# First operands of an output projection made ahead of the last norm, and weight sums moved from GpSimd to VectorE

## Chip, cores and metric

The kernel runs on one core of one Trainium2 chip. The metric is the device time of one execution in microseconds (us); lower is better. A second, profiled execution gives the trace that the rows below are from.

## Reference

One step of a hybrid layer over 2048 prompt tokens and 64 sample tokens (8 sequences of 8), model width 1024, float32. The normed input goes through one projection; three head groups (an SSD scan, gated linear attention, sliding-window attention) each give a part of a 1024-wide mix; the mix goes through `w_out`, and a gated embedding is added. What matters here is the end:

```python
y = (y.reshape(Bsz, L, SSD_WIDTH) * jax.nn.silu(z))
y_ssd = rmsnorm(y.reshape(Bsz, L, 2, 256), ssd_norm_w.reshape(2, -1)).reshape(Bsz, L, SSD_WIDTH)
...
mix = jnp.concatenate([y_ssd, y_gla, y_swa], axis=-1) @ w_out      # 512 + 256 + 256 -> 1024
h = h + mix
h = h + jax.nn.sigmoid(h @ w_pg) * (p @ w_pe)
```

## The kernel before

**Stages.** Tokens are 16 tiles of 128 in 8 blocks of 256; the 64 sample tokens make a 17th tile. Linear attention, window attention and the SSD come first, with tokens in the free dimension; the SSD norm of a block (`s_norm`, L1297 to L1317) is the last thing that its mix needs. Mixes are stored to DRAM (`mixd0` to `mixd16`) and come back in the output stage ("o", L1487 on). The gate stage ("g") follows it.

**Products.** Float32 is kept by splitting each operand into two fp32r parts, high (ScalarE, L1505) and low (VectorE, L1506), with three matmuls for a product of blocks. The output stage takes tiles in pairs and multiplies the 256x1024 mix of a pair by the 1024x1024 `w_out` in the manner of Strassen: seven products a pair, P1 A11·B11, P6 S2·T2, P7 S3·T3, P5 S1·T1, P4 A22·T4, P2 A12·B21, P3 S4·B22, each of 12 matmuls of 128x128 by 128x512. The sample tile alone is a group of four (P1, P6, P2, P3). There are nine groups (pair 0, sample, pairs 1 to 7): 60 products. A11, A12, A21, A22 are quarters of the mix, S1 to S4 their sums (L1563 to L1574: on VectorE for pair 0, on GpSimd for the others). A11 and A21 are the SSD halves, the part that waits for the norm; pair 0 is of block 0, whose norm is long done. Its operands S3, S1 and A22, however, lie in box X9, which the last block's SSD values hold (X_S in the trace) until they are stored to `mixd14` and `mixd15`. Products end in four PSUM banks: X (P1, P2), Y (P6), Z (P7, P4), V (P5, P3); the sums with the residual `h` are at L1534 and L1535 and at L1585, on GpSimd for the sum of P1 and P6 (three adds of 128x512 a group), on VectorE otherwise. A bank's second product starts when the add of its first has read it.

**Weight sums.** T1 to T4 are sums of quarters of `w_out` (and of `w_pg` for the gate), made ahead and kept in DRAM: `t_sums` (L1394 to L1413) goes through eight rounds, each four loads of 128x256 (tile `quads`), four subtractions on GpSimd (L1405, L1406, L1408, L1409; tile `sums`) and four stores (`gT`, `oT`). For `w_pg` this runs beside the output stage.

**What sets the order.** `class Order` lists the work for all engines in advance. Dense units (`od.unit`) keep their order; the generators in `od.chain` are stepped whenever their time is due by the figures that they yield (cost, latency) or by the table `LAT`. Each engine then takes its instructions in the order of that list, except that the scheduler behind it moves them a little. SyncE issues all loads and stores in one row, and a store there that waits for its data holds what is behind it. `c_second` (L1731) loads `h` of the first two groups and makes S3, S1 and A22 of pair 0; `c_weights` (L1476) loads and splits the weights of `w_out`; `last_weights` does B22. All tiles of a phase share boxes of memory named in its plan (`Phase`, L943 for the SSD).

Of the kernel before, what the change touches and what calls it, by code (L numbers as in the profile page):

```python
# [12 lines left out]
AF = mybir.ActivationFunctionType  # L13
# [136 lines left out]
def hybrid_step(ctx: ExitStack, tc: tile.TileContext, I, C, O):  # L150
# [780 lines left out]
    def swa_tiles(odd):  # L931
# [12 lines left out]
        xr1 xr2 xr3:X8; sones afs:Y0; xc:Y0 X9; par2 cdp decs:Y0; sst0 sst1 sst2 sst3 cio:Y1; S0s:Y1 Y1; ab:Y2 Y2; zs rr:Y2;  # L944
# [167 lines left out]
    def u_z(b, m):  # L1112
# [8 lines left out]
        V.scalar_tensor_tensor(out=zss[b][:, m], in0=th[:, 0], scalar=1.0, in1=pf, op0=ALU.add, op1=ALU.mult)  # L1121
        if m == 3:
            od.mark(("z", b), 0.8)
            used(2 * NB + b)
            if b == NB - 1:
                c_weights(2)
# [170 lines left out]
    def s_norm(b):  # L1297
        n = ncols(b)
        yield 0, 0, ("z", b), *[("ch", t[0]) for t in tiles_of(b)]
        y, zs = xcs[b][:, 0:4], zss[b]  # L1300
        V.tensor_tensor(out=y, in0=y, in1=zs, op=ALU.mult)
        A.activation(out=zs, in_=y, func=AF.Square)
        G.tensor_tensor(out=zs[:, 0:4:2], in0=zs[:, 0:4:2], in1=zs[:, 1:4:2], op=ALU.add)
        rr = s1.tile([128, 2, n], F32, tag="rr", name="rr")
        yield 0.9 if n == 256 else 1.1, LAT["y2"] if b < NB - 1 else 3.0
# [88 lines left out]
    def t_sums(w, pause, *needs):  # L1394

        yield 0, 0, *needs
        for k in range(4):
            for c in (0, 256):
# [138 lines left out]
    class Out(Square):  # L1537
# [39 lines left out]
        def unit(self, g, n):  # L1577
# [26 lines left out]
            if G_[0] in self.h:  # L1604
                adds()
            else:
                self.late.append(adds)
# [136 lines left out]
    seq = [(0, 0), (0, 1), (1, 0), (0, 5), (1, 1), (0, 2), (0, 3), (0, 4), (1, 2), (0, 6), (1, 3)]  # L1744
# [121 lines left out]
```

## Time and profile before

| | us |
|---|---|
| median of three runs | 1233.59 (1233.57, 1233.59, 1239.47) |
| profiled execution | 1243.2 |
| its span (first to last instruction) | 1241.4 |
| PE busy | 1181.1 (95%) |
| VectorE busy (DVE) | 711.8 (57%) |
| ScalarE busy (ACT) | 484.2 (39%) |
| GpSimd busy (POOL) | 464.6 (37%) |

The profiled execution lies 9.6 us above the median. Busy shares are means over unlike stages; the stage that the change works in is the output stage, from 812.7 to 1003.9 us of the span, with the gate stage behind it to the end.

### The profile page before, as it was taken

Reading aid. Unit: us, or ns where it says so; the run is one execution under the profiler, and the core shown is the slowest. Engines: PE = TensorE matmul, PEld = TensorE weight load, DVE = VectorE, ACT = ScalarE, POOL = GpSimd, SP = SyncE. Lnnn points to the kernel's source line nnn. Section 1 sums busy time; section 2 is a strip of 40 time slices with the busy share of each in tenths; the row PEclk is TensorE's granted clock in tenths of the full one; section 3 lists DMA queues with packets and bytes.
Section 4 is the critical chain, followed back from the end, with each engine's and each line's share of the span. In section 5 each row is a group of like instructions: output and inputs, shape, how many; then the busy total and the mean of one; then the engine's idle time right before and its main releaser. Section 6 shows DMA issues by size and latency. Waiting matters only on the chain.

```text
span 1241.4 us, 20938 instructions
## 1 busy us (share of the span) xinstructions
PE 1181.1 (95%) x8010; PEld 991.3 (80%) x8010; DVE 711.8 (57%) x1442; ACT 484.2 (39%) x993; POOL 464.6 (37%) x537
## 2 busy tenths in 40 slices
PE   7899999998999998999899999889998999999998
PEld 6787887687888887988798988757776878688886
DVE  4665565745544356568666658866745674344552
ACT  4443433542344346333345535453222352233331
POOL 4222324214411124436334444334877323333331
PEclk8899999999999999998999999999999999999999
DMA  8645465285632256422512343456677432322221
GB/s 251 224 173 191 153 238 160 72 253 158 211 120 99 86 179 200 170 74 80 172 60 95 120 136 112 152 174 202 210 260 261 153 128 70 102 77 77 87 83 51
DMA packets 119036, 182.33 MB, mean 147 GB/s; under 512 B 35573, under 2 KB 88293, under 8 KB 112792
## 3 DMA queue, kind: packets, MB, share of 16 engines
q1 hardware_dynamic: 118936, 180.99, 44.2%
q8 instruction: 63, 1.03, 0.3%
q14 instruction: 37, 0.30, 0.1%
HBM read 125.59 MB, written 55.37 MB: 146 GB/s over the span
## 4 chain that ended last, share of the span: by engine, by line
PE 58%; DMA 14%; DVE 11%; ACT 5%; POOL 4%; issue 4%; SPq 3%; POOLq 0%; DVEq 0%; ACTq 0%
PE pT L205 9%; PE pg L205 5%; PE pfz L205 5%; PE pfx L205 4%; PE pXg L1529 4%; PE peC L205 4%; PE pVg L1529 4%; PE pZg L1529 3%; PE po L205 2%; PE pq L205 2%; PE pYg L1529 2%; DMA quads<-in_w_pg_dram 2%; PE pys L205 2%; DMA raw<-in_w_in_dram 1%; DMA Y_S<-afd 1%
## 5 line engine op out<-in xcount | busy, mean ns | idle before, releaser
L205 PE MATMUL pfx<-uh,w 128*128 128x256 f32 (+1 forms) x768 | 153.1, 294 | 3.8 <-ACT X_S L1094 2.5
L205 PEld LDWEIGHTS pfx<-uh,w 128*128 128x128 f32 x768 | 123.8, 193 | 8.7 <-ACT X_S L1094 3.2
L205 PE MATMUL pfx<-ul,w 128*128 128x256 f32 (+1 forms) x384 | 111.0, 289 | 0.0
L205 PE MATMUL pfz<-uh,w 128*128 128x256 f32 (+1 forms) x512 | 105.4, 298 | 4.2 <-DVE Y_S L1121 3.4
L205 PE MATMUL pg<-uh,w 128*128 128x256 f32 (+1 forms) x512 | 103.4, 294 | 1.6 <-DVE Y_W L891 1.6
L1683 POOL TENSOR_TENSOR X_C<-ul_D,X_C 128x512 f32<-128x512 f32 (+1 forms) x33 | 43.0, 1303 | 135.5 <-DVE ul_D L1682 112.0
L205 PEld LDWEIGHTS pfz<-uh,w 128*128 128x128 f32 x512 | 84.8, 197 | 7.1 <-DVE Y_S L1121 4.2
L205 PE MATMUL pT<-w,uh 128*128 128x512 f32 (+1 forms) x272 | 87.9, 400 | 0.0
L205 PEld LDWEIGHTS pg<-uh,w 128*128 128x128 f32 x512 | 83.2, 193 | 4.6 <-DVE Y_W L891 2.2
L205 PE MATMUL pfz<-ul,w 128*128 128x256 f32 (+1 forms) x256 | 75.4, 294 | 0.0
L205 PEld LDWEIGHTS pfx<-ul,w 128*128 128x128 f32 x384 | 74.0, 193 | 1.5 <-issue 1.3
L205 PE MATMUL pg<-ul,w 128*128 128x256 f32 (+1 forms) x256 | 74.9, 293 | 0.0
L205 PE MATMUL pT<-Y_G,uh 128*128 128x280 f32 (+1 forms) x272 | 62.7, 314 | 3.8 <-ACT uh L326 3.5
L229 DVE TENSOR_TENSOR w<-raw,w 128x1024 fp32r<-128x1024 f32 x32 | 46.6, 1466 | 27.4 <-ACT w L227 27.3
L227 ACT ACTIVATE w<-raw 128x1024 fp32r<-128x1024 f32 x40 | 41.6, 1056 | 49.8 <-DMA raw<-in_w_in_dram 21.5
L205 PEld LDWEIGHTS pT<-w,uh 128*128 128x128 f32 (+1 forms) x272 | 48.8, 185 | 12.1 <-issue 1.8
L1506 DVE TENSOR_TENSOR uh_C<-ul_C,uh_C 128x512 fp32r<-128x512 f32 (+1 forms) x35 | 33.5, 967 | 39.9 <-ACT uh_C L1505 39.9
L1682 DVE SCALAR_TENSOR_TENSOR ul_D<-ul_D,peC 128x512 f32<-128x512 f32 (+1 forms) x34 | 23.3, 685 | 54.1 <-PE peC L205 46.1
L1529 PE MATMUL pZo<-w,X_C 128*128 128x512 f32 x192 | 48.3, 401 | 6.0 <-DVE X_C L1585 6.0
L205 PE MATMUL pT<-w,ul 128*128 128x512 f32 (+1 forms) x136 | 53.9, 397 | 0.0
L205 PE MATMUL peC<-Y_P,uh_C 128*128 128x512 f32 (+1 forms) x204 | 52.8, 393 | 0.8 <-DVE ul_D L1682 0.8
L1505 ACT ACTIVATE uh_C<-ul_C 128x512 fp32r<-128x512 f32 (+1 forms) x35 | 20.8, 609 | 81.2 <-POOL ul_C L1574 31.2
(437 smaller groups left out, 3045.5 us busy)
## 6 DMA issues: line engine op xcount, KB each, us to landing
uh<-uhd SPq DMA_DIRECT2D x14, 1024.0 KB
ul<-uld SPq DMA_DIRECT2D x14, 1024.0 KB
raw<-in_w_in_dram SPq DMA_DIRECT2D x17, 512.0 KB
X_G<-in_x_prompt_dram SPq DMA_DIRECT2D x16, 512.0 KB
Y_S<-afd SPq DMA_DIRECT2D x16, 512.0 KB
X_C<-in_x_prompt_dram SPq DMA_DIRECT2D x16, 512.0 KB
ul_C<-mixd SPq DMA_DIRECT2D x16, 512.0 KB
out_y_prompt_dram<-X_C SPq DMA_DIRECT2D x16, 512.0 KB
```

The lines of the kernel that those rows point to most:

```text
L205: PE.matmul(out, lhsT=lhsT, rhs=rhs, start=start, stop=stop)
L227: A.activation(out=hi[:, k0:k1], in_=rw, func=AF.Copy, scale=scale)
L229: eng.tensor_tensor(out=lo[:, k0:k1], in0=rw, in1=hi[:, k0:k1].bitcast(F32), op=ALU.subtract)
L1505: A.activation(out=t[:, 0, :, :R], in_=src, func=AF.Copy)
L1506: eng.tensor_tensor(out=t[:, 1, :, :R], in0=src, in1=t[:, 0, :, :R].bitcast(F32), op=ALU.subtract)
L1529: PE.matmul(ps[:R], lhsT=a[:, x, k, :R], rhs=b[:, y + k], start=first and k + i == 0, stop=k == 3 and i == 2, skip_group_check=True)
L1682: V.scalar_tensor_tensor(out=th, in0=th, scalar=1.0, in1=pe[:R], op0=ALU.add, op1=ALU.mult)
L1683: eng.tensor_tensor(out=h[:R, cs], in0=th, in1=h[:R, cs], op=ALU.add)
```

## The change

- In the SSD's plan the two boxes of `xc` change places, so that the last block's values lie in Y0 and the block before that in X9.
- The norm of the last block takes its product with the gate and its squares in two halves, the first after two of the four z units; the second half's sum of squares goes from GpSimd to VectorE. The planner's latency of the norm falls from 6.9 and 3.0 to 2.5 for the last two blocks.
- `c_second` stands right behind the last z unit and needs only the end of the scan. It takes the loads of T1 and T4 along, which stood in the last z unit.
- The first eleven products stand in another order, and the operands of group 2 are made in two parts.
- The sums of `w_pg` go from GpSimd to VectorE, and from a chain with due times to steps taken at fixed products: 34 steps, one after each product of groups 2 to 6 but the first (four steps a round), with no condition on their end but an assertion.

```diff
-        xr1 xr2 xr3:X8; sones afs:Y0; xc:Y0 X9; par2 cdp decs:Y0; sst0 sst1 sst2 sst3 cio:Y1; S0s:Y1 Y1; ab:Y2 Y2; zs rr:Y2;
+        xr1 xr2 xr3:X8; sones afs:Y0; xc:X9 Y0; par2 cdp decs:Y0; sst0 sst1 sst2 sst3 cio:Y1; S0s:Y1 Y1; ab:Y2 Y2; zs rr:Y2;
...
+        if m == 1:
+            od.mark(("z1", b), 0.8)
         if m == 3:
             od.mark(("z", b), 0.8)
             used(2 * NB + b)
-            if b == NB - 1:
-                c_weights(2)
...
-        yield 0, 0, ("z", b), *[("ch", t[0]) for t in tiles_of(b)]
-        y, zs = xcs[b][:, 0:4], zss[b]
-        V.tensor_tensor(out=y, in0=y, in1=zs, op=ALU.mult)
-        A.activation(out=zs, in_=y, func=AF.Square)
-        G.tensor_tensor(out=zs[:, 0:4:2], in0=zs[:, 0:4:2], in1=zs[:, 1:4:2], op=ALU.add)
+
+        for i, m in enumerate((2, 4) if b == NB - 1 else (4,)):
+            last = m == 4
+            yield 0, 0, ("z" if last else "z1", b), *[("ch", t[0]) for t in tiles_of(b)]
+            y, zs = xcs[b][:, 0:4], zss[b]
+            h = slice(2 * i, m)
+            V.tensor_tensor(out=y[:, h], in0=y[:, h], in1=zs[:, h], op=ALU.mult)
+            A.activation(out=zs[:, h], in_=y[:, h], func=AF.Square)
+            (V if i else G).tensor_tensor(out=zs[:, 2 * i:m:2], in0=zs[:, 2 * i:m:2], in1=zs[:, 2 * i + 1:m:2], op=ALU.add)
         rr = s1.tile([128, 2, n], F32, tag="rr", name="rr")
-        yield 0.9 if n == 256 else 1.1, LAT["y2"] if b < NB - 1 else 3.0
+        yield 0.9 if n == 256 else 1.1, LAT["y2"] if b < NB - 2 else 2.5
...
-                yield 0, pause
+                yield
+                yield
                 t = stg.tile([128, 4, 256], F32, tag="raw", name="sums")
-                G.tensor_tensor(out=t[:, 0], in0=q[:, 1], in1=q[:, 0], op=ALU.subtract)
-                G.tensor_tensor(out=t[:, 1], in0=q[:, 3], in1=t[:, 0], op=ALU.subtract)
-                yield 0, 2.5
-                G.tensor_tensor(out=t[:, 2], in0=q[:, 3], in1=q[:, 1], op=ALU.subtract)
-                G.tensor_tensor(out=t[:, 3], in0=q[:, 2], in1=t[:, 1], op=ALU.subtract)
-                yield 0, pause - 3.0
+                E.tensor_tensor(out=t[:, 0], in0=q[:, 1], in1=q[:, 0], op=ALU.subtract)
+                E.tensor_tensor(out=t[:, 1], in0=q[:, 3], in1=t[:, 0], op=ALU.subtract)
+                yield
+                E.tensor_tensor(out=t[:, 2], in0=q[:, 3], in1=q[:, 1], op=ALU.subtract)
+                E.tensor_tensor(out=t[:, 3], in0=q[:, 2], in1=t[:, 1], op=ALU.subtract)
+                yield
...
-seq = [(0, 0), (0, 1), (1, 0), (0, 5), (1, 1), (0, 2), (0, 3), (0, 4), (1, 2), (0, 6), (1, 3)]
+seq = [(0, 0), (0, 1), (0, 2), (0, 5), (1, 0), (1, 1), (0, 3), (0, 4), (0, 6), (1, 2), (1, 3)]
...
-preps = {(0, 0): "1 A11", (0, 5): "1 A12", (0, 6): "1 S4", (0, 4): "2 A11 S2 S3 S1 A22", (1, 2): "2 A12", (1, 3): "2 S4"}
+preps = {(0, 0): "1 A11", (0, 5): "1 A12", (0, 6): "1 S4", (1, 1): "2 A11 S2", (0, 4): "2 S3 S1 A22", (1, 2): "2 A12", (1, 3): "2 S4"}
+
+gs = t_sums("g", V)
...
         if (g, n) == (2, 0):
             e_weights()
-            od.mark("summing", 6.0)
+        elif 2 <= g < last - 1:
+            next(gs, None)
...
+            if n == 0:
+                assert next(gs, "end") == "end"
             operand("g", *late[n])
 
     od.unit(0, c_mid, ("U", 3 * NB - 1))
+    od.unit(0, c_second, "ssd")
     for g, n in seq:
-        od.unit(2.73, partial(o_unit, g, n), ("o", co.prods(g)[n][2]), *([("sums", "g")] if g == last else []))
-        if (g, n) == (0, 5):
-            od.unit(0, c_second, ("norm", NB - 1), "ssd", "cstate")
+        od.unit(2.73, partial(o_unit, g, n), ("o", co.prods(g)[n][2]))
```

How the rows of the engines move, at three places. In these rows a name is box, phase and a number (`X9_C`: box X9, output stage; `_S`: SSD), then the shape; the lines of the changed kernel are ten further on in the output stage, four to five in the SSD.

**The last norm and pair 0's operands.** VectorE, before: the last norm's final step is L1312; L1506 on X9_C is the low part of S3, S1 and A22.

```order
L1585 TENSOR_TENSOR X7_C_8878<-pXo_8826,X7_C_8878 64x512
L1506 TENSOR_TENSOR uh_C_8787<-ul_C_8592,uh_C_8787 128x512
L1312 SCALAR_TENSOR_TENSOR X9_S_5228<-X9_S_5228,Y0_S_3525,Y2_S_5188 128x256 x4
L1535 TENSOR_TENSOR ul_C_8785<-ul_C_8785,pYo_8893 64x512
L1506 TENSOR_TENSOR uh_C_8595<-ul_C_8592,uh_C_8595 128x512
L229 TENSOR_TENSOR Y2_C_8863<-raw_8864,Y2_C_8863 128x1024
L229 TENSOR_TENSOR Y2_C_8863<-raw_8868,Y2_C_8863 128x1024
L1506 TENSOR_TENSOR X9_C_8884<-ul_C_8592,X9_C_8884 128x512 x3
```

VectorE, after (L1305 is the norm's product, in halves; L1316 its final step; L1516 on X9_C the low parts):

```order
L1305 TENSOR_TENSOR Y0_S_3525<-Y0_S_3525,Y2_S_5189 128x512
L1290 COPY Y2_S_5189<-ptf_8694 128x256
L1516 TENSOR_TENSOR X9_C_8801<-ul_C_8592,X9_C_8801 128x512
L1331 COPY Y2_S_5189<-ptx_8737 3x384
L1516 TENSOR_TENSOR X9_C_8801<-ul_C_8592,X9_C_8801 128x512 x2
L1121 SCALAR_TENSOR_TENSOR Y2_S_5189<-X6_S_5154,pfz_8707 128x256
L1331 COPY Y2_S_5189<-ptx_8702 3x384
L229 TENSOR_TENSOR w512_8783<-raw_8784,w512_8783 128x1024
L229 TENSOR_TENSOR w512_8783<-raw_8788,w512_8783 128x1024
L1121 SCALAR_TENSOR_TENSOR Y2_S_5189<-X7_S_5196,pfz_8743 128x256
L1516 TENSOR_TENSOR uh_C_8772<-ul_C_8592,uh_C_8772 128x512
L1305 TENSOR_TENSOR Y0_S_3525<-Y0_S_3525,Y2_S_5189 128x512
```

The low parts of S3, S1 and A22 (X9_C) stood behind the norm's last step and stand now ahead of the norm's second half, among the z units (L1121).

SyncE at the same place, before (`mixd16` is the sample mix, in `ul_C`):

```order
L1315 DMA mixd12_115<-Y0_S_3525 128x4x128
L1315 DMA mixd13_116<-Y0_S_3525 128x4x128
L1293 DMA out_ssm_prompt_dram<-Y2_S_5188 128x64 x4
L1543 DMA ul_C_8785<-mixd16_119 128x8x64
L1499 DMA X6_C_8875<-in_x_prompt_dram 128x1024 x2
L1543 DMA ul_C_8785<-mixd5_108 128x1024
L226 DMA raw_8771<-oT4_216 128x1024
```

SyncE, after:

```order
L1319 DMA mixd12_115<-X9_S_5081 128x4x128
L1319 DMA mixd13_116<-X9_S_5081 128x4x128
L1293 DMA out_ssm_prompt_dram<-Y2_S_5189 128x64 x4
L1553 DMA ul_C_8592<-mixd3_106 128x1024
L1509 DMA X6_C_8778<-in_x_prompt_dram 128x1024
L1332 DMA out_conv_prompt_dram<-Y2_S_5189 3x768
L1553 DMA ul_C_8770<-mixd16_119 128x8x64
```

The load of the sample mix stood right behind the final state's stores; now the load of `mixd3` (into the buffer that S3, S1 and A22 are made from), a load of `h` and a store of the convolution state are ahead of it.

**The first products.** PE, before, from the end of the last z unit (`pXo`, `pYo`, `pZo`, `pVo`: the four banks; 64x512: the sample group; `pn`: the last norm's sum over partitions):

```order
L1529 MATMUL pXo_8793<-w512_8155,uh_C_8595 128x512 x12
L1529 MATMUL pYo_8811<-w512_8394,uh_C_8595 128x512 x12
L1529 MATMUL pXo_8793<-Y1_C_8164,uh_C_8787 128x512 x2
L1529 MATMUL pXo_8826<-w512_8155,uh_C_8595 64x512 x2
L1529 MATMUL pXo_8793<-Y1_C_8164,uh_C_8787 128x512 x10
L1529 MATMUL pXo_8826<-w512_8155,uh_C_8595 64x512 x10
L1529 MATMUL pXo_8826<-Y1_C_8164,uh_C_8787 64x512 x12
L205 MATMUL pn_8839<-Y2_S_5188,Y0_S_3525 128x512
L1529 MATMUL pYo_8893<-w512_8394,uh_C_8595 64x512 x12
L1529 MATMUL pXo_9018<-w512_8155,uh_C_8595 128x512 x12
L1529 MATMUL pZo_8909<-w512_8403,X9_C_8884 128x512 x2
```

PE, after:

```order
L1539 MATMUL pYo_8828<-w512_8394,uh_C_8595 128x512 x12
L1539 MATMUL pXo_8810<-w512_8155,uh_C_8595 128x512 x12
L1539 MATMUL pXo_8897<-w512_8155,uh_C_8595 64x512 x12
L1539 MATMUL pXo_8810<-Y1_C_8164,uh_C_8772 128x512 x3
L205 MATMUL pn_8846<-Y2_S_5189,Y0_S_3525 128x512
L1539 MATMUL pZo_8856<-w512_8403,X9_C_8801 128x512 x12
L1539 MATMUL pXo_8810<-Y1_C_8164,uh_C_8772 128x512 x9
L1539 MATMUL pYo_8910<-w512_8394,uh_C_8595 64x512 x12
L1539 MATMUL pVo_8933<-w512_8783,X9_C_8801 128x512 x12
L1539 MATMUL pZo_8856<-w512_8792,X9_C_8801 128x512 x12
L1539 MATMUL pXo_8897<-Y1_C_8164,uh_C_8772 64x512 x12
```

Ahead of `pn` stand now P6, P1 and the start of P2 of pair 0 and the sample's P1, and P7 of pair 0 (`pZo`) right behind it, with P5 and P4 three products later. Before, P7 of pair 0 stood behind P1 and P2 of both groups, `pn`, the sample's P6 and group 2's P1.

**The weight sums.** GpSimd, before, at the first rounds (L1405 to L1409 the sums; L1563 to L1574 sums of the mix; L1585 adds to `h`):

```order
L1405 TENSOR_TENSOR sums_9155<-quads_9102 128x256
L1408 TENSOR_TENSOR sums_9155<-quads_9102 128x256
L1565 TENSOR_TENSOR ul_C_8592<-ul_C_8592 128x512
L1406 TENSOR_TENSOR sums_9155<-quads_9102,sums_9155 128x256
L1574 TENSOR_TENSOR ul_C_8592<-ul_C_8592 128x512
L1563 TENSOR_TENSOR ul_C_8592<-ul_C_8785 128x512
L1409 TENSOR_TENSOR sums_9155<-quads_9102,sums_9155 128x256
L1564 TENSOR_TENSOR ul_C_8785<-ul_C_8785 128x512
L1565 TENSOR_TENSOR ul_C_8785<-ul_C_8592,ul_C_8785 128x512
L1585 TENSOR_TENSOR X6_C_8875<-ul_C_8785,X6_C_8875 128x512 x2
L1405 TENSOR_TENSOR sums_9274<-quads_9222 128x256
```

VectorE, after, at two of the later rounds (L1410 to L1414 the same sums):

```order
L1595 TENSOR_TENSOR X6_C_8778<-pZo_9367,X6_C_8778 128x512
L1516 TENSOR_TENSOR X9_C_8801<-ul_C_8770,X9_C_8801 128x512
L1410 TENSOR_TENSOR sums_9608<-quads_9571 128x256
L1595 TENSOR_TENSOR X6_C_8778<-pVo_9385,X6_C_8778 128x512
L1516 TENSOR_TENSOR X9_C_8801<-ul_C_8592,X9_C_8801 128x512
L1411 TENSOR_TENSOR sums_9608<-quads_9571,sums_9608 128x256
L1413 TENSOR_TENSOR sums_9608<-quads_9571 128x256
L1414 TENSOR_TENSOR sums_9608<-quads_9571,sums_9608 128x256
L1595 TENSOR_TENSOR X6_C_8778<-pZo_9367,X6_C_8778 128x512
L1410 TENSOR_TENSOR sums_9696<-quads_9659 128x256
L1595 TENSOR_TENSOR X6_C_8778<-pXo_9322,X6_C_8778 128x512
```

The four subtractions of a round left GpSimd, whose rows in these groups are now L1573 to L1584 and L1595 alone, and stand on VectorE between the adds that free the banks (L1595) and the low parts (L1516).

## Rows read from the trace of the kernel before

**Rows 1.** Windows: stretch, us, busy of PE, PEld, DVE, ACT, POOL, granted clock, DMA share, GB/s.
```profile
812.70:1003.90 191.20, 174.10 (x740) 136.61 (x738) 115.18 (x134) 62.36 (x93) 110.52 (x88) 0.97 0.64 212
812.70:867.00 54.30, 46.80 (x185) 33.12 (x183) 33.73 (x39) 22.56 (x31) 22.11 (x16) 0.94 0.63 197
867.00:1003.90 136.90, 127.29 (x556) 103.49 (x555) 81.45 (x95) 39.80 (x62) 88.41 (x72) 0.99 0.65 217
1003.90:1241.00 237.10, 230.10 (x1081) 184.67 (x1079) 109.16 (x166) 71.76 (x130) 74.91 (x58) 1.00 0.24 82
```
**Rows 2.** Waits of PE, 805 to 1005 us: total us, times, longest us.
```profile
PE pZo L1529 <- DVE X_C L1585: 6.0, 3, 3.0
PE pXo L1529 <- ACT ul_C L1534: 4.1, 2, 2.9
PE pYo L1529 <- DVE uh_C L1506: 2.3, 1, 2.3
```
**Rows 3.** Timeline of PE: start, us, what, matmuls [idle before <- releaser].
```profile
812.74 3.00 PE L1529 MATMUL pXo<-w,uh_C 128*128 128x512 f32 x12
...
828.33 4.22 PE L1529 MATMUL pXo<-Y_C,uh_C 128*64 128x512 f32 x12 [2.91 <-ACT ul_C L1534]
832.35 1.42 PE L205 MATMUL pn<-Y_S 128*128 128x512 f32 x2
833.20 3.09 PE L1529 MATMUL pYo<-w,uh_C 128*64 128x512 f32 x11
...
867.03 2.88 PE L1529 MATMUL pVo<-w,X_C 128*128 128x512 f32 x12
869.75 2.88 PE L1529 MATMUL pXo<-w,uh_C 128*128 128x512 f32 x12
...
955.20 4.61 PE L1529 MATMUL pZo<-w,X_C 128*128 128x512 f32 x12 [2.99 <-DVE X_C L1585]
```
**Rows 4.** Timeline of SyncE's queue, ScalarE and VectorE about the last norm.
```profile
814.79 0.58 SPq L1543 DMA_DIRECT2D ul_C<-mixd  x1
...
818.67 0.42 ACT L1505 ACTIVATE uh_C<-ul_C 128x256 fp32r<-128x256 f32 x1 [3.30 <-DMA ul_C<-mixd]
...
836.77 1.67 DVE L1312 SCALAR_TENSOR_TENSOR X_S<-X_S,Y_S 128x256 f32<-128x256 f32 x4 [2.90 <-ACT Y_S L1310]
...
841.76 1.67 ACT L1505 ACTIVATE X_C<-ul_C 128x512 fp32r<-128x512 f32 x3 [1.15 <-DMA mixd<-X_S]
```
**Rows 5.** Chain of waits, 780 to 1010 us: start, us, what.
```profile
818.02 8.70 DMA raw<-oT
...
885.86 4.65 DMA quads<-in_w_pg_dram
```
**Rows 6.** Windows around two stalls of PE, columns as in rows 1.
```profile
837.00:842.00 5.00, 3.05 (x8) 2.14 (x9) 4.95 (x8) 2.50 (x4) 1.66 (x1) 0.80 0.34 105
953.00:958.00 5.00, 2.80 (x8) 2.29 (x9) 4.46 (x5) 1.98 (x4) 4.36 (x3) 0.80 1.00 371
```
**Rows 7.** Waits of GpSimd and VectorE, 805 to 1005 us.
```profile
POOL sums L1405 <- DMA quads<-in_w_pg_dram: 12.9, 5, 4.6
...
DVE X_C L1585 <- POOL X_C L1585: 6.6, 2, 5.2
```
**Rows 8.** Groups by line and shape, 867 to 970 us: busy us, mean ns | idle before.
```profile
L1585 POOL TENSOR_TENSOR X_C<-ul_C,X_C 128x512 f32<-128x512 f32 x16 | 25.0, 1585 | 1.0 <-DVE ul_C L1535 1.0
...
L1406 POOL TENSOR_TENSOR sums<-quads,sums 128x256 f32<-128x256 f32 x7 | 6.9, 984 | 2.6 <-DMA quads<-in_w_pg_dram 2.6
```
**Rows 9.** Timeline of VectorE and GpSimd: VectorE alone, and beside GpSimd.
```profile
799.15 0.69 DVE L1563 TENSOR_TENSOR ul_C<-ul_C 128x512 f32<-128x512 f32 x1
...
801.03 1.29 POOL L1163 TENSOR_TENSOR X_S<-X_S 128x512 f32<-128x512 f32 x1 [2.50 <-DMA X_S<-ead]
801.50 1.37 DVE L1564 TENSOR_TENSOR ul_C<-ul_C 128x512 f32<-128x512 f32 x1
...
860.67 0.41 DVE L1506 TENSOR_TENSOR uh_C<-ul_C,uh_C 128x256 fp32r<-128x256 f32 x1
```

More of the change, by code (lines that the diff above doesn't have):

```diff
@@ L1392, in hybrid_step, with t_sums @@
     t_d = {(w, t): tc.dram_tile([128, 4, 512], F32, name=f"{w}{t}") for w in "og" for t in ("T1", "T2", "T3", "T4")}
-    def t_sums(w, pause, *needs):
-        yield 0, 0, *needs
+    def t_sums(w, E):
+        t = None
         for k in range(4):
@@ L1402, in t_sums, with o_sums @@
                         SP.dma_start(out=q[ps, i], in_=s)
-                yield 0, pause
+                yield
+                yield
                 t = stg.tile([128, 4, 256], F32, tag="raw", name="sums")
-                G.tensor_tensor(out=t[:, 0], in0=q[:, 1], in1=q[:, 0], op=ALU.subtract)
-                G.tensor_tensor(out=t[:, 1], in0=q[:, 3], in1=t[:, 0], op=ALU.subtract)
-                yield 0, 2.5
-                G.tensor_tensor(out=t[:, 2], in0=q[:, 3], in1=q[:, 1], op=ALU.subtract)
-                G.tensor_tensor(out=t[:, 3], in0=q[:, 2], in1=t[:, 1], op=ALU.subtract)
-                yield 0, pause - 3.0
+                E.tensor_tensor(out=t[:, 0], in0=q[:, 1], in1=q[:, 0], op=ALU.subtract)
[4 more added lines that the diff above has]
+                yield
                 for i in range(4):
                     SP.dma_start(out=t_d[w, f"T{i + 1}"][:, k, c:c + 256], in_=t[:, i])
-        od.mark(("sums", w))
+    def o_sums():
+        yield 0, 0, "wg", ("qk", 0)
+        for i, _ in enumerate(t_sums("o", G)):
+            yield 0, (5.5, 5.5, 2.5, 8.0)[i % 4]
+        od.mark(("sums", "o"))
     ws = {}
@@ L1486, in __init__ @@
         def __init__(self, w, groups, sets):
-            self.w, self.groups, self.sets, self.late = w, groups, sets, []
+            self.w, self.groups, self.sets = w, groups, sets
             self.mx, self.h, self.op, self.ps, self.pt, self.r = {}, {}, {}, {}, {}, {}
@@ L1602, in adds @@
                     SP.dma_start(out=h_d[i][:R], in_=self.h[i][:R])
[L1604 to L1607, printed above, removed]
+            adds()
             if g > 1:
@@ L1733, in c_second @@
         co.load_h(1)
-        for f in co.late:
-            f()
+        c_weights(2)
         for key in ("S3", "S1", "A22"):
@@ L1780, in hybrid_step @@
             od.unit(3.5, partial(cg.unit, g, n), ("g", cg.prods(g)[n][2]))
-    od.chain(t_sums("o", 11.0, "wg", ("qk", 0)))
-    od.chain(t_sums("g", 6.0, "summing"))
+    od.chain(o_sums())
     od.chain(last_weights())
```

## Prediction

> **What bounds the kernel now.** I read the windows first. From 812.7 us on the kernel is the output stage (191.2 us to the first gate product) and the gate stage (237.1 us) [rows 1]. In the gate stage PE is busy 230.1 of 237.1 us, so what the output stage saves or loses reaches the end. Next the timeline of PE: undisturbed products start 2.72 us apart (867.03, 869.75) [rows 3], and 60 of them would take 163.2 us. The stage takes 191.1, so 28 us are lost in it. Third, where: the first 15 products end at 867.0, 54.3 us for 40.8, 13.5 lost; the other 45 take 136.9 for 122.4, 14.5 lost [rows 1, 3]. Of these, idle PE is 54.3 - 46.8 = 7.5 and 136.9 - 127.3 = 9.6 [rows 1]; the rest is products that ran longer. Fourth, the waits of PE say who is waited for: the adds that free banks Z (6.0) and X (4.1), and an operand's low part (2.3) [rows 2]. After each such wait the granted clock is 0.80 over five us [rows 6]: part of the stretch at 1.2 GHz instead of 2.4. A window of 5 us at 0.80 has lost 5 x 0.20 = 1.0 us, and a product right behind a wait took 4.22 or 4.61 in place of 3.00 [rows 3]. So a wait costs itself and 1.0 to 1.6 more.
>
> **Head: what goes.** Before, pair 0's P7 cannot start until S3 is made, and S3 lies where the last block's SSD values lie. The last norm's step ends at 838.4, its store must have read them, and the copies of S3, S1 and A22 start at 841.8 [rows 4], 29 us into the stage. PE meanwhile has only P1, P2 and P6 of both groups, and waits between them, since two products share bank X (2.91 at 828.33) [rows 3]. The change gives the last block's values another box, so S3, S1 and A22 depend on the block before, whose norm is done during the z units; their rows stand ahead of the last norm's second half. P7, P5 and P4 can fill the gaps, and no operand of pair 0 is late. This is the edit with one answer: the 13.5 us are the pot.
>
> **Head: what is late next.** On SyncE the sample mix's load now stands behind the load of mixd3, which waits until VectorE has read S3, S1 and A22 from its buffer, and behind a load of h and a store that waits for VectorE. Before, it was issued at 814.79, and the sample's A11 began at 818.67, 3.9 us later [rows 4]. After, I set its issue at 815 to 816, about a z unit later, so A11's high part (0.42) and low part are ready at 820 to 821.3. PE has P6 and P1 of pair 0 first and comes to the sample's P1 at 812.74 + 2 x 2.72 = 818.2. It waits 1.9 to 3.1; I take 2.5. Bounds: 1 if SyncE gets through faster, 4 if the convolution store (its data come from VectorE) holds it. Nothing can pass, as PE goes in order. Behind the wait the clock costs 1.0 to 1.6, I take 1.5. The norm's matmuls `pn` stay: 0.85 from their start to the next product's (832.35 to 833.20) [rows 3]. Together 4.9 lost where 13.5 were: **8.6 gained**, between 13.5 - 0.85 - 1.0 = 11.7 (wait of 1, no clock loss) and 13.5 - 0.85 - 4 - 1.6 - 2 = 5.0, where the last 2 stand for a late T4 or pn. T4's load, second half, lands at 826.7 before [rows 5]; its place on SyncE hardly moves and its split takes some 3 us more, while P4 stands ninth on PE and cannot start before 812.74 + 8 x 2.72 = 834.5. B22 is needed later still. So these are covered by 5 us or more. The norm in halves and the sum on VectorE shorten a chain that nobody waits for any more (block 7's mix is needed in the last group); their cost is nothing while that holds, and if pn were late PE would stand, which the 2 covers.
>
> **The other groups: what goes.** Of the 9.6 idle, 2.3 is group 2's operand S2, late because of the head [rows 2]; its operands are now begun two products earlier. 6.0 is bank Z's add [rows 2]. Its releaser is VectorE's add, which is itself behind GpSimd's three adds to the same h (6.6 in two waits), and GpSimd is held by the weight sums: its subtractions wait 12.9 us for the quads [rows 7]. A longest case of 2.99 at 955.20 [rows 3] is a load of h queued on SyncE behind stores of the sums, which wait for GpSimd. With the sums off GpSimd, all four subtractions of a round (four of about 0.98 [rows 8], 3.9 us) and their waits leave it; in this stretch it is busy 88.4 of 136.9 us [rows 1], and the 32 subtractions are 31 of these 88. The h adds (1.585 each [rows 8]) then follow P6 at once. The remaining 1.3 (9.6 - 6.0 - 2.3) is at the turn to the gate and stays. So 8.3 idle can go, and with three waits 1.0 each of clock: 11.3 at most.
>
> **The other groups: what comes.** VectorE gets 32 subtractions of 128x256. One such operation took 0.41 alone [rows 9], 13 us in all; it has 136.9 - 81.5 = 55 us free [rows 1]. Beside GpSimd the same 128x512 operation took 1.37, alone 0.69 [rows 9]; doubled, the 32 take 26 us, and still fit. What does not fit as easily is order: VectorE takes its rows in turn, so a subtraction that waits for its quads holds the bank's add behind it. On GpSimd such waits were 12.9 in five, 2.6 in the mean and 4.6 at most [rows 7]; the loads themselves take 4.65 [rows 5]. In the new order they are issued two products (5.4 us) ahead of their use, so most are in. I take one wait that reaches PE, 2.6 and 1.0 of clock, and 0.9 that is left of the late h load, whose queue still has the stores in it. **Gain 11.3 - 4.5 = 6.8**, between 0 (four such waits, or the next rival) and 11.3. The condition on the sums ahead of the last group is gone from the list, which costs nothing: the last step stands at the last round's product.
>
> The Trainium skill speaks against this edit: "SBUF — State Buffer", section "Who interferes with whom", says that a VectorE instruction with two SBUF inputs and a GpSimd instruction that reads SBUF exclude each other, so that one is blocked until the other ends. The trace agrees so far as it goes: 1.37 beside GpSimd against 0.69 [rows 9]. By it VectorE would not be given GpSimd's time for nothing.
>
> **Sum.** The profiled run took 1243.2 (span 1241.4 and 1.8 around it); 8.6 + 6.8 = 15.4 makes 1227.8. The median is 9.6 below the profiled run; I take it that both lose the same in these stalls, so the median becomes 1233.6 - 15.4 = **1218.2, say 1218**. The other phases (813 us) keep their order but for boxes and the earlier norm of block 6, and I cost them at nothing: the first write into the new boxes waits for VectorE work that is long done.
>
> **Rivals.** (A) All of it hides: no new wait in the head but pn, none from the quads. 1233.6 - 11.7 - 11.3 = 1210.6, with one wait left about 1212. For it: products are issued with two products of slack. Against: SyncE's order is there to be read, and the sample's load is in it.
>
> (B) VectorE and GpSimd block each other. If each of the 32 subtractions waits for a GpSimd operation of 0.98 [rows 8], they take 32 x 1.4 = 45 us of VectorE's 55 free, and GpSimd is held in turn; adds of banks come late again and the later groups gain nothing: 1233.6 - 8.6 = 1225.0 (1224 to 1227). For it: the pair in [rows 9]. Against: GpSimd would then be busy 57 of 137 us, so that most subtractions meet nothing.
>
> (C) The 9.6 us by which the profiled run is above the median lie in these very stalls, so that a usual run has less to save: 15.4 - 9.6 = 5.8, 1227.8; or the sample's load takes 4 and more and the steady gain is 0: 1233.6 - 5.0 = 1228.6. Against the first: most of these waits follow from the order of instructions, which is the same in each run.
>
> (D) Slower: VectorE is held in each of eight rounds by quads, as GpSimd was, with an add for PE behind it. By the longest wait, 8 x 4.6 = 36.9 [rows 7]: 1233.6 - 15.4 + 36.9 = 1255. It decides from (15.4 + 6.2) / 8 = 2.7 us a round reaching PE. For it: DMA is at 0.65 busy in this stretch and at 1.00 around 955 [rows 1, 6]. Against: the loads are issued two products ahead, GpSimd's chain issued them as its due times came, and PE's banks allow one product of delay.
>
> **How the numbers follow.** 0.5% (6.2 us) is about what a measurement of this kernel can tell from no change. Forecast, 1212 to 1224: 0.50. A, 1209 to 1212: 0.10. B, 1224 to 1227.4: 0.16. C, 1227.4 to 1234: 0.16. D, over 1239.8: 0.08, of which little lies below. Faster (under 1227.4) is 0.50 + 0.10 + 0.16 = 0.76, same 0.16, slower 0.08. The range leaves out D, half of A and a part of C: 1211 to 1229.
>
> **What would show it.** In the changed profile: the copies of S3, S1 and A22 start before 815, not at 841.8; PE's first wait in the stage is for the sample's A11, about 2.5 at 818; 15 products take some 46 us instead of 54.3. In the later groups no row of sums is left on GpSimd, PE's waits for bank Z's add fall from 6.0 to under 3, VectorE shows waits for quads, and the stage takes about 176 us. Wrong would be: a wait for T4 or pn in the head, subtractions well over 1 us on VectorE with PE waiting for adds, or more than 2.7 us of PE's waits a round behind quads.

## The result, and the profile after

| | before | changed |
|---|---|---|
| median, 14 runs each (us) | 1237.65 | 1227.34 |
| profiled execution, span (us) | 1241.4 | 1222.0 |
| ahead of the output stage (us) | 812.7 | 803.3 |
| output stage, first product to first gate product (us) | 191.1 | 181.0 |
| of it the first 15 products / the other 45 (us) | 54.3 / 136.8 | 44.8 / 136.2 |
| gate stage, to the end of the span (us) | 237.6 | 237.7 |

The ratio of the times is 0.9915, 95% interval 0.9889 to 0.9941: 7.3 to 13.7 us faster, where 15.4 were forecast. The time lies in the stated range. The median of before is now 4 us above that of the three runs which the forecast started from. The spans differ by 19.4 us, of which 9.5 lie ahead of the output stage. A second profile of the changed kernel reaches its output stage at 808.4, so that part moves between executions of one program, and I don't count it. The stage itself is 10.1 us shorter; the second profile has 179.9. So differences of about 1 us between stages, each of one profile, say nothing.

Windows of the changed kernel (stretch, us, busy of PE, PEld, DVE, ACT, POOL, clock, DMA share, GB/s; PE is TensorE's matmuls, PEld its weight loads), to be laid beside [rows 1]:

```profile
803.20:984.30 181.10, 169.47 (x739) 134.94 (x739) 121.16 (x164) 60.11 (x89) 84.08 (x55) 0.99 0.68 221
803.20:848.00 44.80, 42.60 (x185) 31.69 (x185) 32.47 (x45) 21.94 (x31) 22.80 (x14) 1.00 0.80 258
848.00:984.30 136.30, 126.87 (x555) 103.25 (x555) 88.69 (x120) 38.17 (x58) 61.29 (x42) 0.99 0.64 209
```

The head (the first 15 products) is 9.5 us shorter and its granted clock is at 1.00 instead of 0.94. In the other 45 products GpSimd is busy 61 us instead of 88 and VectorE 89 instead of 81, as meant, but PE is idle 9.4 us instead of 9.6: nearly nothing is gained there. The timeline of PE says where it stands, with [rows 3] beside it:

```profile
803.26 2.91 PE L1539 MATMUL pYo<-w,uh_C 128*128 128x512 f32 x12
...
810.36 0.68 PE L1539 MATMUL pXo<-w,uh_C 128*64 128x512 f32 x2 [1.47 <-ACT uh_C L1515]
811.77 2.50 PE L1539 MATMUL pXo<-w,uh_C 128*64 128x512 f32 x10 [0.73 <-DVE uh_C L1516]
...
815.26 3.31 PE L1539 MATMUL pZo<-w,X_C 128*128 128x512 f32 x12
...
845.32 2.88 PE L1539 MATMUL pVo<-w,X_C 128*128 128x512 f32 x12
...
853.46 3.02 PE L1539 MATMUL pZo<-w,X_C 128*128 128x512 f32 x12 [2.54 <-DVE X_C L1595]
...
875.97 4.54 PE L1539 MATMUL pZo<-w,X_C 128*128 128x512 f32 x12 [3.62 <-DVE X_C L1595]
```

P7 of pair 0 (pZo, 815.26) starts 12.0 us into the stage, where it stood at 30.9. The only wait of the head is the sample's P1, 1.47 + 0.73 = 2.2 us. In the later groups come waits for bank Z's add as before, now 2.54 and 3.62; the wait for S2, 2.3 before, is gone, and 1.8 for bank V came.

Waits of PE and VectorE in the changed kernel, 800 to 986 us (total, times, longest); the third row answers to the first of [rows 7]:

```profile
PE pZo L1539 <- DVE X_C L1595: 6.2, 2, 3.6
...
PE pVo L1539 <- DVE X_C L1595: 1.8, 2, 1.4
...
DVE sums L1410 <- DMA quads<-in_w_pg_dram: 17.8, 6, 6.2
```

GpSimd's wait for the quads, 12.9 us, is now VectorE's, 17.8 us, and bank Z's wait is 6.2 where it was 6.0 [rows 2]. How the one makes the other, in the timelines of VectorE and GpSimd:

```profile
871.13 0.43 DVE L1410 TENSOR_TENSOR sums<-quads 128x256 f32<-128x256 f32 x1 [6.16 <-DMA quads<-in_w_pg_dram]
...
872.79 0.68 DVE L1545 TENSOR_TENSOR ul_C<-ul_C,pYo 128x512 f32<-128x512 f32 x1
...
873.55 4.56 POOL L1595 TENSOR_TENSOR X_C<-ul_C,X_C 128x512 f32<-128x512 f32 x3 [7.15 <-DVE ul_C L1545]
...
875.23 0.69 DVE L1595 TENSOR_TENSOR X_C<-pZo,X_C 128x512 f32<-128x512 f32 x1 [1.15 <-POOL X_C L1595]
```

VectorE stands 6.16 us before a subtraction. Behind it in its row is L1545, the sum of banks X and Y, for which GpSimd's three adds to h wait 7.15; behind the first of these is bank Z's add, and PE's 3.62.

### The profile page after: what moved, and what is told of

Its sections match the earlier page's. It is cut to its first block, busy times and chain, and to the rows that moved or that the text cites. A ratio compares the mean times of both kernels' runs of the same rounds, so it can differ in the third digit from the quotient of the medians.

```text
span 1222.0 us, 20943 instructions
## 1 busy us (share of the span) xinstructions
PE 1168.4 (96%) x8010; PEld 983.9 (81%) x8010; DVE 720.3 (59%) x1476; ACT 484.4 (40%) x994; POOL 441.8 (36%) x505
## 5 line engine op out<-in xcount | busy, mean ns | idle before, releaser
L205 PE MATMUL pfz<-uh,w 128*128 128x256 f32 (+1 forms) x512 | 102.8, 293 | 3.9 <-DVE Y_S L1121 2.5
L205 PEld LDWEIGHTS pfz<-uh,w 128*128 128x128 f32 x512 | 82.3, 191 | 7.0 <-DVE Y_S L1121 3.3
L1689 DVE SCALAR_TENSOR_TENSOR ul_D<-ul_D,peC 128x512 f32<-128x512 f32 (+1 forms) x34 | 23.3, 685 | 53.7 <-PE peC L205 48.1
L205 PEld LDWEIGHTS pT<-Y_G,uh 128*128 128x128 f32 (+1 forms) x272 | 46.2, 197 | 7.5 <-ACT uh L326 3.6
L205 PEld LDWEIGHTS pg<-ul,w 128*128 128x128 f32 x256 | 49.3, 193 | 0.9 <-issue 0.4
```

Of the source, the lines that this page charges most:

```text
L205: PE.matmul(out, lhsT=lhsT, rhs=rhs, start=start, stop=stop)
L1689: V.scalar_tensor_tensor(out=th, in0=th, scalar=1.0, in1=pe[:R], op0=ALU.add, op1=ALU.mult)
```

## Experiments

Each kernel was timed in five rounds beside the kernel before. The stage is that of its one profile, from the first product to the first gate product; the last column splits it where 15 products are done. "Head alone" is the changed kernel with the sums of `w_pg` left on GpSimd as before. The times tell the large steps apart; differences of 0.3% between the versions near 0.99 lie within their intervals, and there the stage and its waits are read. The first 15 products run from 43.9 to 48.1 us in kernels with the same head, by the clock behind one wait, so that the sums are judged by the other 45.

| kernel | ratio (95%) | stage | first 15 / other 45 |
|---|---|---|---|
| changed, second profile | 0.9905 (0.9873 to 0.9938) | 179.9 | 44.0 / 136.0 |
| head alone | 0.9878 (0.9844 to 0.9912) | 176.7 | 46.2 / 130.5 |
| sums alone | 1.0019 (0.9998 to 1.0041) | 193.4 | 57.4 / 136.0 |
| sums at fixed products, on GpSimd | 0.9888 (0.9854 to 0.9922) | 176.6 | 43.9 / 132.7 |
| one product more of slack | 0.9891 (0.9855 to 0.9927) | 179.0 | 44.1 / 135.0 |
| head alone, old order | 0.9891 (0.9860 to 0.9923) | 177.5 | 45.7 / 131.8 |
| head alone, old boxes | 0.9998 (0.9974 to 1.0023) | 187.4 | 55.1 / 132.3 |
| changed, no quads read | 0.9917 (0.9892 to 0.9943) | 180.5 | 48.1 / 132.5 |
| own buffers, VectorE | 0.9861 (0.9833 to 0.9888) | 176.3 | 46.4 / 129.9 |
| own buffers, GpSimd | 0.9899 (0.9876 to 0.9922) | 176.5 | 43.9 / 132.7 |
| head alone, norm in one piece | 0.9907 (0.9880 to 0.9933) | 180.5 | 50.2 / 130.3 |
| own buffers, sample's mix early | 0.9880 (0.9853 to 0.9908) | 175.3 | 45.7 / 129.6 |

**The two halves of the change.** Head alone:

```diff
-    gs = t_sums("g", V)
+    def g_sums():
+        yield 0, 0, "summing"
+        for i, _ in enumerate(t_sums("g", G)):
+            yield 0, (3.0, 3.0, 2.5, 3.0)[i % 4]
+        od.mark(("sums", "g"))
...
-        elif 2 <= g < last - 1:
-            next(gs, None)
+            od.mark("summing", 6.0)
...
+    od.chain(g_sums())
```

> The changed kernel with the sums of w_pg put back on GpSimd, as a chain with the due times of before; only the head (boxes, norm in halves, early operands, order of the first products) is changed. Theory 1 (the whole gain is the head; moving the sums only moved the wait for the quads from GpSimd to VectorE): first 15 products 44.8 us as in the changed kernel, the other 45 within 1.5 us of 136.3, time 1227 +- 2 where before has 1237.7. Theory 2 (the sums' move does give some 6 us, and something in the new head takes them back from the later groups): the later 45 products take 140 us or more, time 1232 to 1235.

Sums alone (the kernel before with these lines, the head as it was):

```diff
+    gs = t_sums("g", V)
...
-            od.mark("summing", 6.0)
+        elif 2 <= g < last - 1:
+            next(gs, None)
...
```

> The kernel before with only the sums of w_pg moved to VectorE, at the same fixed products; the head is that of before. Theory 1: no change, 1236 to 1239, the first 15 products 54.3 us, VectorE waiting for quads 15 us and more. Theory 2: 1230 to 1232, the later 45 products near 130 us.

Theory 1 holds, and more than it said: the head alone takes the stage from 191.1 to 176.7 us, 14.4, and the time to 0.9878, about 15 us; the sums alone make it 193.4 and change no time that can be measured. Both halves of the stage gain from the head: 8.1 us in the first 15 products and 6.3 in the other 45, which the expectation had not seen. PE's waits in the head alone, 800 to 990 us:

```profile
PE pZo L1539 <- DVE X_C L1595: 2.6, 2, 1.3
PE pXo L1539 <- ACT uh_C L1515: 1.5, 1, 1.5
...
PE pXo L1539 <- ACT ul_C L1544: 1.3, 2, 0.8
```

Bank Z's wait is 2.6 here, though the subtractions are on GpSimd as before; GpSimd's waits ahead of them for the quads fell from 12.9 to 8.6 us in six. The same waits in the sums alone:

```profile
PE pYo L1535 <- DVE uh_C L1512: 4.8, 1, 4.8
...
PE pVo L1535 <- DVE X_C L1591: 2.2, 3, 1.5
PE pZo L1535 <- DVE X_C L1591: 2.0, 1, 2.0
```

The 2.0 for bank Z lie in the first 15 products. In the other 45 no wait for bank Z is left, so with the sums off GpSimd the waits went that were to go; but S2 is waited for 4.8 instead of 2.3 (which also gives the adds behind it more time), and 2.2 came for bank V, so that these 45 still take 136.0. Either half takes most or all of the 6.0 away; only with the head does time come of it. That GpSimd's wait for quads did reach PE, the kernel before shows in its timelines of GpSimd, VectorE and PE:

```profile
890.68 0.74 POOL L1405 TENSOR_TENSOR sums<-quads 128x256 f32<-128x256 f32 x1 [4.61 <-DMA quads<-in_w_pg_dram]
891.37 4.21 POOL L1585 TENSOR_TENSOR X_C<-ul_C,X_C 128x512 f32<-128x512 f32 x3
...
892.68 0.69 DVE L1585 TENSOR_TENSOR X_C<-pZo,X_C 128x512 f32<-128x512 f32 x1 [5.22 <-POOL X_C L1585]
...
893.52 2.99 PE L1529 MATMUL pZo<-w,X_C 128*128 128x512 f32 x12 [0.61 <-DVE X_C L1585]
```

The 4.61 us become VectorE's 5.22, but only 0.61 of PE. The sums alone also wait for quads on VectorE, 17.1 us in seven.

**Engine or place.** The changed kernel with one letter changed:

```diff
-    gs = t_sums("g", V)
+    gs = t_sums("g", G)
```

> The changed kernel with the sums at the same fixed products, but on GpSimd. It tells the engine from the place in the order. If the engine matters (VectorE's bank adds stand behind the waits for quads): PE's waits for bank adds fall, the 45 products take 132 us or less, time 1223. If the place matters alone: as the changed kernel, 1227. If GpSimd's queue is the worse place, since three adds of h stand behind the waits: 140 us or more, 1231 and up.

The engine: at the same products but on GpSimd the other 45 take 132.7 us instead of 136.2, the stage is 176.6, and PE waits for bank adds 2.0 (Z) and 2.0 (V). So of the 5.7 us between the changed kernel and the head alone 3.5 go with the engine; the other 2.2 go with the fixed products in place of due times. Its time, 0.9888 (0.9854 to 0.9922), cannot be told from the changed kernel's, so the 3 to 4 us show in the stage and not in the time. A second profile of the changed kernel was to tell whether they are chance:

> The changed kernel itself, on the chip and in the call of the three others, for a second look at its stage. If the 4.3 us between it and the head alone in the output stage are the sums' place on VectorE and not chance, its stage is 180 to 182 us again and its later 45 products take 135 to 137; by chance alone it could as well be 176 to 178.

179.9 and 136.0: the 45 products came out within 0.3 us of the first profile, so by these two they are not.

**What on VectorE costs it.** More slack:

```diff
                 yield
                 yield
+                if w == "g":
+                    yield
                 t = stg.tile([128, 4, 256], F32, tag="raw", name="sums")
```

(and none between the two pairs of subtractions).

> The changed kernel with a third product between the loads of the quads and the subtractions (all four subtractions then in one step), the same number of steps. If the wait of VectorE for the quads sets the loss of the later groups: the waits of the first subtraction (17.8 us in six in the changed kernel) fall below 8, PE's waits for bank adds from 9.4 to 5 or less, time 1222 to 1224. If it is the slowing of VectorE's operations beside GpSimd's (0.41 to 1.5 us): the waits for quads fall, but PE still waits 8 us or more and the time stays at 1226 to 1228.

Inconclusive: the waits fell only to 15.3 us in five, and the other 45 products took 135.0. The loads are held too: on SyncE they stand behind the stores of the round before, and in the later groups the stores waited 14.6 us, in seven, for a round's first subtraction on VectorE. The next kernel takes the quads out of the subtractions, so that its sums are not those of `w_pg`:

```diff
-                E.tensor_tensor(out=t[:, 0], in0=q[:, 1], in1=q[:, 0], op=ALU.subtract)
...
+                q = q if w == "o" else [wes[0].rearrange("p a b -> p (a b)")[:, 256 * j:256 * j + 256].bitcast(F32) for j in range(4)]
+                q = [q[:, j] for j in range(4)] if w == "o" else q
+                E.tensor_tensor(out=t[:, 0], in0=q[1], in1=q[0], op=ALU.subtract)
...
```

> The changed kernel with subtractions that read a resident tile in place of the quads; loads, stores and all instructions stay, the sums are not those of w_pg, so the gate's result is left out. It takes VectorE's wait for the quads away and leaves the work of VectorE beside GpSimd. Theory Q (the waits for quads cost the later groups what the sums' move lost): no waits for quads, the later 45 products fall from 136.3 to 130 to 132, stage 175 to 177. Theory L (VectorE and GpSimd slow each other): the subtractions keep means of 0.6 to 1.0 us with single ones of 1.5, PE still waits 7 us or more for bank adds, stage 180 or more.

The other 45 fall to 132.5 us, near the 130 to 132 of theory Q, but the run does not decide, since VectorE's waits did not go. The stage stays at 180.5, since in this profile the head took 48.1, with a longer stretch at the lower clock behind the sample's P1 (0.93 over the first 15 products). Waits of VectorE, 800 to 990 us, then one of them on VectorE and on PE:

```profile
DVE sums L1412 <- DMA gT<-sums: 10.7, 5, 6.3
...
DVE sums L1412 <- DMA quads<-in_w_pg_dram: 7.4, 2, 4.2
```

```profile
885.59 0.42 DVE L1412 TENSOR_TENSOR sums<-Y_P 128x256 f32<-128x256 f32 x1 [6.31 <-DMA gT<-sums]
...
887.80 5.43 PE L1541 MATMUL pVo<-Y_C,uh_C 128*128 128x512 f32 x12 [4.31 <-DVE X_C L1597]
```

VectorE's waits ahead of L1412 are 18.1 us in all, as much as the 17.8 of the changed kernel: a subtraction that reads no quads now waits, mostly for the stores of the round before, 6.31 us at the longest. PE meets them twice behind the head, 1.0 and 4.3. `quads` and `sums` share two staging buffers, so a round's sums can be written only when the last round's have been stored, and its quads be loaded only when the last ones are used. If this recycling is the cause, buffers of their own must take it away. The next kernel has them; it also asks for a round's quads one round ahead, and for the embedding's weights (`e_weights`) only behind the sums:

```diff
+        qk = Phase("Q", boxes, "qd:Y0 Y0; sm:Y0 Y0")
...
+        nxt = load(0)
+        for r in range(8):
+            q, k, c = nxt, r // 2, r % 2 * 256
+            yield
+            if r < 7:
+                nxt = load(r + 1)
+            yield
+            t = qk.tile([128, 4, 256], F32, tag="sm", name="sums")
...
```

> The changed kernel, the sums still on VectorE at fixed products, but with two buffers of their own for the quads and two for the sums (in box Y0, which is free there; the embedding's weights are loaded after the sums), and the quads of a round asked for one round ahead. Stage 181.0 and 179.9 us in the changed kernel, 176.6 to 177.5 with the sums on GpSimd. Theory W (VectorE's waits for a round's loads and stores cost the later groups): these waits fall from 17 us to under 4, PE's waits for bank adds from 6 to 9 us to under 4, stage 173 to 176. Theory L (VectorE and GpSimd slow each other): waits go, PE's waits stay at 6 or more, stage 179 to 181.

Theory W holds for the later groups: they take 129.9 us, 6 less than in the changed kernel, with the subtractions on the same engine. Not all of it is saved: 12 of the 32 subtractions now stand in the first 15 products, where 4 stood. VectorE still waits 9 us for its data, where under 4 were expected, but 3.3 at the longest, and PE but once for bank Z. The waits of PE and VectorE, 800 to 986 us:

```profile
DVE Y_Q L1439 <- DMA Y_Q<-in_w_pg_dram: 4.7, 4, 1.8
...
DVE Y_Q L1440 <- DMA Y_Q<-in_w_pg_dram: 3.3, 1, 3.3
...
PE pZo L1568 <- DVE X_C L1624: 2.4, 1, 2.4
```

The stage is 176.3 and not 173 to 176, by a head of 46.4. How much of this is the buffers and how much the earlier loads was not taken apart. On GpSimd with the same buffers:

> The same with the subtractions on GpSimd. Theory W: no better than on VectorE, 173 to 176 for the stage, since with the data there in time either engine has room. If GpSimd's load by itself holds the bank adds (three adds to h of 1.6 us behind four subtractions of 0.9 us): PE still waits 3 to 5 us and the stage is 176 to 178.

The second case: bank adds still wait (4.2 in three for Z, 0.8 for V), the other 45 take 132.7. That is what it was with shared buffers (132.7), so on GpSimd neither the buffers nor the later embedding weights gain anything there. With the data there in time VectorE is the better place, by 2.8 us of the other 45 products; with shared buffers it was the worse, by 3.5. Over the whole stage the two differ by 0.2 us only, since the head took 46.4 with the one and 43.9 with the other.

**The parts of the head.** Old order of the first eleven products and old operands of group 2:

```diff
-    seq = [(0, 0), (0, 1), (0, 2), (0, 5), (1, 0), (1, 1), (0, 3), (0, 4), (0, 6), (1, 2), (1, 3)]
+    seq = [(0, 0), (0, 1), (1, 0), (0, 5), (1, 1), (0, 2), (0, 3), (0, 4), (1, 2), (0, 6), (1, 3)]
...
-    preps = {(0, 0): "1 A11", (0, 5): "1 A12", (0, 6): "1 S4", (1, 1): "2 A11 S2", (0, 4): "2 S3 S1 A22", (1, 2): "2 A12", (1, 3): "2 S4"}
...
+    preps = {(0, 0): "1 A11", (0, 5): "1 A12", (0, 6): "1 S4", (0, 4): "2 A11 S2 S3 S1 A22", (1, 2): "2 A12", (1, 3): "2 S4"}
...
```

> The head alone (sums of w_pg on GpSimd as before), with the order of the first eleven products and the operands of group 2 as before: what is left are the boxes, the norm in halves and the early operands. Output stage 191.1 us before, 181.0 in the changed kernel, 176.7 with the whole head alone. Theory 1 (the boxes and early operands carry it): stage 177 to 180, the first 15 products 45 to 48, time 1225 to 1229 where before has 1238 to 1240. Theory 2 (the new order carries it, since group 2's operands come earlier): stage 184 to 188, the later 45 products 135 and more, time 1232 to 1236.

Old boxes (of the SSD's plan only the entry of `xc`):

```diff
-... xc:X9 Y0; ...
+... xc:Y0 X9; ...
```

> The whole head alone, but with the two boxes as before: S3, S1 and A22 of pair 0 again wait for the last block's store, although their instructions stand early. Theory 1 (the boxes are what frees them): PE waits 5 us and more ahead of the first product of bank Z, stage 188 to 195, time 1235 to 1243. Theory 2 (the norm in halves ends so early that the boxes hardly matter): stage 178 to 182, time 1226 to 1230.

Norm in one piece:

```diff
-        for i, m in enumerate((2, 4) if b == NB - 1 else (4,)):
+        for i, m in enumerate((4,)):
...
-        yield 0.9 if n == 256 else 1.1, LAT["y2"] if b < NB - 2 else 2.5
+        yield 0.9 if n == 256 else 1.1, LAT["y2"] if b < NB - 1 else 3.0
```

> The head alone (sums on GpSimd as before, stage 176.7), with the last two norms in one piece and with the latencies of before; boxes, early operands and order stay. The last norm's sums over partitions then come later on PE than in halves. If nobody waits for that norm any more: stage within 1.5 us of 176.7. If PE meets its matmuls before their data: a wait of 2 us or more ahead of pn, stage 179 to 183.

The order is worth 0.8 us of stage, nothing that one profile or the time can show. The boxes are worth most: without them the ratio is 0.9998 and the stage 10.7 us longer than the head alone, just under the 188 expected, and PE waits for S3 again, 4.2 us where 5 and more were expected (its timeline, P7 of pair 0):

```profile
829.41 1.22 PE L1539 MATMUL pZo<-w,X_C 128*128 128x512 f32 x2 [4.21 <-ACT X_C L1515]
```

The norm in halves with its latencies is worth 3.8 us of stage. Its 180.5 lies in the 179 to 183 of the second case, but not for its reason: there was no wait ahead of `pn`, and the rest of the list moved with the latencies: at P3 of pair 0 PE waited 3.66 us, with VectorE's add of bank V behind a low part whose sum on GpSimd came 3.85 us late to ScalarE. That it is the list and not the norm's own speed is argued, not shown.

**What is left in the head.** The sample's mix loaded early, into X8, in the version with buffers of its own:

```diff
-... hA:X6 X6; hB:X7 X8; ...
+... hA:X6 X6; hB:X8 X7; ...
...
+                mx = self.mx[g] = ck.tile([128, 1, 8, 64], F32, tag="hB", name="mxs", cap=1024)
...
         co.load_mx(0)
+        co.load_mx(1)
```

> The version with its own buffers for the sums on VectorE (stage 176.3 us), and the sample's mix loaded early into another box (X8), so that its first operand no longer waits for a load that starts when the last z unit ends. That operand still shares its place with pair 0's A11 and can be made only when P1 of pair 0 has ended. If the late load is what PE waits for at its third product (1.8 + 0.4 us in that version, 1.5 to 2.3 in the others): the wait falls to about 1, and with less time at the lower clock the first 15 products take 43 to 45 us, the stage 173 to 175, the time 1220 to 1222 where before has 1238 to 1240. If the shared place is what counts: the wait stays at 1.4 or more and the stage at 176.

The load was the cause: PE's third product now waits 0.28 us.

```profile
814.75 3.22 PE L1568 MATMUL pXo<-w,uh_C 128*64 128x512 f32 x12 [0.28 <-ACT uh_C L1544]
```

The first 15 products take 45.7 us and the stage 175.3, a little over the 43 to 45 and 173 to 175 expected, since 1.96 us came back ahead of the sample's P3; the time, 0.9880, is not better than 0.9861. That the two versions with their own buffers and the sums on VectorE beat the head alone is not shown: 0.4 to 1.4 us of stage is what two profiles of one kernel differ by, and the times overlap. So the sums' move, even with buffers of its own, gained nothing that these runs can tell from the head alone.

## Why the prediction was right, and where not

- **Head, right.** 8.6 us were forecast from boxes that free S3, S1 and A22; measured 9.5, and with the old boxes it is gone (55.1 for the first 15 products, 54.3 before). The copies of the three start at 800.5, ahead of the stage. The wait for the sample's A11 was put at 1.9 to 3.1 us and is 2.2. The clock's price behind it, 1.5 forecast, was near zero in the two profiles of the changed kernel (the granted clock over the first 15 is 1.00), and up to 2.0 in others with the same head (ten matmuls of the sample's P1 took 4.53 in the kernel that reads no quads and 2.50 in the changed kernel).
- **T4, B22 and `pn`, right.** No wait for them in the changed kernel.
- **The other groups, wrong.** 6.8 us were forecast, 0.6 measured. In "what goes" the link from GpSimd's waits to bank Z's is borne out: it is in the trace of before, and with the sums alone bank Z's waits in these groups went. What failed is the step from the waits to a gain. The sums alone gain 0.8 there, since S2 and bank V are waited for instead. And the head alone, with the sums on GpSimd, brings bank Z's wait from 6.0 to 2.6 and gains 6.3, so the gains of the two halves could not be added. A size was off too: 28 of the 32 subtractions lie in this stretch, and GpSimd's busy time fell by 27 us, not 31.
- **What in the head frees the later groups** stays open. With the old boxes they take 132.3 (133.9 with a wait of 1.65 us that stands just ahead of them), with the old order 131.8, with the norm in one piece 130.3, so no one of these carries it. It is not that pair 0 must be on time: with the old boxes it is late. The early place of `c_second`, which all three keep, was not tested alone.
- **What comes, undersized.** One wait behind the quads, 2.6 + 1.0, was taken, with "0" as the lower bound for four such. Measured against the head alone it was 5.7 us (136.2 for 130.5), so the sums' move took back most of what the head gave there. The mechanism is rival D's, VectorE held by quads with PE's add behind it, at 5.7 / 8 = 0.7 us a round, far from the 2.7 from which it would have decided. The loads were thought to be two products ahead; the step did not look at the shared buffers, nor at the stores ahead of the loads on SyncE, and the longest wait is 6.2.
- **Rival B's time, mainly for another reason.** Its result, nothing gained in the later groups, is what came. The blocking is real (below) and made one wait of 2.54 us. With buffers of their own the waits for data shrank and the time came back, but there the 32 subtractions also took less, 16.8 us for 21.1, and the one wait for bank Z that was left, 2.4, stands behind two subtractions of 1.5. So that the blocking is the smaller part is likely, not shown.
- **Rival C.** Its surplus of the profiled run is rather ahead of the stage than in it: the two profiles of the changed kernel differ by 5.1 us there and by 1.1 in the stage, and over all the kernels the output stage starts between 803 and 813 us, while the gate stage agrees within 0.6. The kernel before was profiled only once, so for it this is not shown.
- **The sum.** That the time fell into the range is in part luck: the steps were 8.6 + 6.8, the runs gave 9.5 + 0.6, on a median of before 4 us higher, and a range that was made wide for rivals B and C held both misses. That 15.4 is near what the head alone gives, 14.4 in the stage and about 15 in the time, is chance, since 6.8 of it were laid to the sums.

## What to carry to other kernels

Two edits that claim the same wait must not be added: here either half of the change took most of bank Z's 6.0 us away, and only one of them gave time. The test is to run each half alone, and to look which wait stands in the place of the one that went. When work moves to another engine, its waits move too, and stand there ahead of whatever that engine does for the bottleneck; ask which buffers its loads and stores share, and what its loads stand behind in their queue, before asking how long its instructions are. A tile whose place belongs to something unfinished waits as surely as one whose data are late, and without the swap of two places nearly all of the gain here was gone.

## What the runs showed of the hardware

In these rows VectorE is not slowed by a share: its instructions with two operands in SBUF (the on-chip memory) end just behind the end of one of GpSimd's. The changed kernel, both engines around 846 to 853 us:

```profile
846.76 0.67 DVE L1595 TENSOR_TENSOR X_C<-pVo,X_C 64x512 f32<-64x512 f32 x1
847.36 0.91 DVE L1410 TENSOR_TENSOR sums<-quads 128x256 f32<-128x256 f32 x1
848.20 1.77 DVE L1516 TENSOR_TENSOR uh_C<-ul_C,uh_C 128x512 fp32r<-128x512 f32 x1
849.89 1.50 DVE L1411 TENSOR_TENSOR sums<-quads,sums 128x256 f32<-128x256 f32 x1
851.32 1.49 DVE L1413 TENSOR_TENSOR sums<-quads 128x256 f32<-128x256 f32 x1
852.73 0.68 DVE L1595 TENSOR_TENSOR X_C<-pZo,X_C 128x512 f32<-128x512 f32 x1
...
846.25 3.17 POOL L1595 TENSOR_TENSOR X_C<-ul_C,X_C 128x512 f32<-128x512 f32 x2
849.38 1.74 POOL L1575 TENSOR_TENSOR ul_C<-ul_C 128x512 f32<-128x512 f32 x1
851.08 1.45 POOL L1595 TENSOR_TENSOR X_C<-ul_C,X_C 128x512 f32<-128x512 f32 x1
```

GpSimd's instructions end at 849.42, 851.12 and 852.53; VectorE's (L1516, L1411, L1413) end at 849.97, 851.39 and 852.81, 0.3 to 0.6 us later, a little less than such an instruction takes alone (0.41 for 128x256, 0.69 for 128x512 [rows 9]). So each seems to have run only when GpSimd's had ended. The add from PSUM (the matmuls' banks; L1595) at 846.76, with only one operand in SBUF, takes 0.67 beside GpSimd, and 0.68 at 852.73 when GpSimd has ended. This agrees with the Trainium skill, "SBUF — State Buffer", section "Who interferes with whom", by which an instruction of VectorE with two SBUF inputs contends with one of GpSimd that reads SBUF, for ports that are an exclusive lock, and one with at most one SBUF input does not.
